# Last feed-forward of a two-layer diffusion backbone: second products two d_ff tiles behind, weight halves in another ring

## The chip, the cores and the metric

The kernel runs on one core of a Trainium2 chip. The metric is the time of one launch on the device, in microseconds (us). Five engines work side by side, each in the order of its own queue: TensorE (matrix products; PE in the profile, PEld its weight loads), VectorE (DVE), ScalarE (ACT), GpSimd (POOL) and SyncE (SP), which here issues nearly all transfers from memory. Engines wait for one another by semaphores only.

## The reference, cut to what matters

Two layers work on 256 latent tokens and 256 context tokens of width 1024. A layer is a half-step SwiGLU feed-forward, a token mixer, and another half-step feed-forward, each behind an RMS norm with a learned modulation. After the last layer only the latent tokens are normalised and returned. The change touches the last feed-forward and the final norm behind it:

```python
def rms_norm(x, g):
    y = xf * lax.rsqrt(jnp.mean(xf * xf, axis=-1, keepdims=True) + EPS)
    return y * g

def swiglu(h, w_in, w_out):                 # w_in 1024 x 5632, w_out 2816 x 1024
    g, u = jnp.split(h @ w_in, 2, axis=-1)
    return (jax.nn.silu(g) * u) @ w_out

x = x + 0.5 * mx[8] * swiglu(modulate(rms_norm(x, norm_g[layer, 2]), mx[6], mx[7]), w_in, w_out)
...
return rms_norm(x, final_norm_g)
```

Everything is float32 in the reference.

## The kernel before, in words

**Products in three passes.** A float32 operand is held as a pair: a high part, which is the value rounded to TensorE's fast float32 form by a copy on ScalarE, and a low part, which is the value less the high part, a subtraction on VectorE. `split` (L198, L199) makes the pair; `mm3` (L226 to L228) multiplies high by high, high by low and low by high into one PSUM bank. So each weight tile that comes from memory passes a raw buffer (`weight_raw`, L207), a copy and a subtraction, before TensorE can use it.

**Rings.** Buffers come from rings by tag. `raw` has 3 buffers of 1024 columns for fetched weights. `whi` and `wlo` have 4 each, also of 1024, for the parts of weights. `r2k` is the general ring: 46 buffers of 512 columns, from which activations and their parts come. PSUM has 8 banks. A buffer is given out again when its last reader is done; who gets which is settled when the program is built. A planner also settles the order of the instructions on each engine then: it goes by the program's order and lets a later instruction go first where it believes an earlier one not ready. On the chip each engine then keeps that order.

**The stage ahead.** The attention's output projection (`closing`, with one step for each of 8 blocks of 128 features) adds its result to the residual stream, and as each block of x is finished, `Raw.grown` splits it for the feed-forward (scaled by the norm's gain, without the token's rstd, which is applied to the products later) and adds its square to the sums. `Raw.leading` then multiplies the weights of the first d_ff tile, og and ou, and calls `rstd`: four tiny products of the sums with ones (L239), square root, reciprocal, two transposes (L245) and a copy (L247).

**The last feed-forward**, `last_ffn`, loops over 22 tiles f of 128 d_ff columns. In each step:

- the first products: og (gate) and ou (up), each 8 blocks in 3 passes, 24 products of 258 columns (256 tokens and two columns that carry the shift's product)
- the fetch of 128 rows of w_out (1024 columns, `in_woutn`), their multiplication by the output gate on GpSimd (L912), and their split into one `whi` and one `wlo` buffer
- the second products of an earlier tile, `second` (L906): two token blocks by two halves of 512 output columns by three passes, 12 products of 512 columns that add up in four PSUM banks over all f
- the activations of tile f: end columns copied (L918, L919), products times rstd (L921, L923), Silu (L922), sum and product (L924), and their split into two `r2k` buffers (L926, L927).

`held` is the list of tiles whose second products are to come. Before the change the loop empties it in each step, ahead of the step's own activations, so that the second products stand one tile behind, but step 20 leaves it alone; step 21 then does tiles 19 and 20, and tile 21 follows after the loop. In steps 5, 7, 9 and 11 the residual x is added to the four banks by products with the identity (L932). After the loop come the final norm's squares (L941), root, scaling and the two stores for each half of the tokens.

The raw buffers are asked for in the order og, ou, w_out of each tile, and SyncE issues the fetches in that order.

Of the kernel before, what the change touches and what calls it, by code (L numbers as in the profile page):

```python
# [19 lines left out]
KT = D // P  # L20
# [3 lines left out]
NF = DFF // P  # L24
# [13 lines left out]
def hybrid_backbone_kernel(ctx, tc, t, out):  # L38
    nc = tc.nc
# [5 lines left out]
    def bank(shape=(P, 512)):  # L45
        return ps.tile(list(shape), F32, tag="bank", name="bank")

    def r2k(n=512, parts=P):
        return ring.tile([parts, n], F32R, tag="r2k", name="r2k", bufs=46)

    def tmp(n=512, parts=P):
        return ring.tile([parts, n], F32, tag="tmp", name="tmp", bufs=6)
# [4 lines left out]
    def big():  # L57
        return ring.tile([P, 1152], F32R, tag="big", name="big", bufs=4)

    def small(n=4):  # L60
        return ring.tile([P, n], F32, tag="small", name="small", bufs=24)
# [28 lines left out]
    def behind(ins):  # L90

        return tc.issue_after(ins.ins) if ins else nullcontext()
# [102 lines left out]
    def split(hi, lo, src, bias=None, engine=nc.vector):  # L195

        if bias is None:
            nc.scalar.copy(hi, src)  # L198
            return engine.tensor_tensor(lo, src, hi.bitcast(F32), ALU.subtract)  # L199
        else:  # L200
            nc.scalar.activation(hi, src, AF.Identity, bias=bias)
            return nc.vector.scalar_tensor_tensor(lo, src, bias, hi.bitcast(F32), ALU.add, ALU.subtract)  # L202

    def weight_raw(ap, n=1024, raw=None):
        if raw is None:
            raw = ring.tile([P, 1024], F32, tag="raw", name="wraw", bufs=3)
        nc.sync.dma_start(raw[:, :n], ap)  # L207
        return raw[:, :n]
# [4 lines left out]
    def weight_split(raw, engine=nc.vector, after=None):  # L213
        n = raw.shape[1]
        hi = ring.tile([P, 1024], F32R, tag="whi", name="whi", bufs=4)
        lo = ring.tile([P, 1024], F32R, tag="wlo", name="wlo", bufs=4)
        with behind(after):
            split(hi[:, :n], lo[:, :n], raw, engine=engine)
        return hi[:, :n], lo[:, :n]

    def mm3(o, terms, which=None, n=None):

        n = n or len(terms)
        for i in range(n) if which is None else which:
            (ah, al), (bh, bl) = terms[i]
            nc.tensor.matmul(o, lhsT=ah, rhs=bh, start=(i == 0), stop=False)  # L226
            nc.tensor.matmul(o, lhsT=ah, rhs=bl, start=False, stop=False)  # L227
            nc.tensor.matmul(o, lhsT=al, rhs=bh, start=False, stop=(i == n - 1))  # L228
# [42 lines left out]
    class Sublayer:  # L271
# [61 lines left out]
        def leading(self, s):  # L333


            self.product(self.lead[:self.both], s)
            if len(self.streams) > 1 and s == 0:
                self.r[1] = self.rstd(1)
            for i in range(self.both, len(self.first)):
                if i == len(self.lead):  # L340
                    ap, size = self.first[i]
                    self.lead.append((weight(ap, size, after=self.end), bank(), size // KT))
                self.product(self.lead[i:i + 1], s)
# [65 lines left out]
    def ffn_specs(l, which):  # L409
        return [(t["win"][l, which, f, u], 1024) for f in range(NF) for u in range(2)]  # L410
# [422 lines left out]
    class Raw(Sublayer):  # L833
# [20 lines left out]
        def leading(self, s):  # L854
            for k in range(KT):
                for wt, o, M in self.lead:
                    mm3(o[:M, :self.W], self.terms(wt, M), (k,))
            _, self.r = self.rstd(s)

        def products(self, specs):  # L860
            for i, (ap, size) in enumerate(specs):
# [28 lines left out]
    def last_ffn(sl):  # L890


        fngr = big().bitcast(F32)[:, :1024]
        nc.sync.dma_start(fngr, t["fngr"])
        outs = sl.products(ffn_specs(1, 1))
        acc = [[bank() for _ in range(2)] for _ in range(2)]
        r = sl.r
        held = []

        def second(f, gu, w):  # L900
            for i in range(2):
                rows = slice(i * P, (i + 1) * P)
                for h in range(2):
                    cols = slice(h * 512, h * 512 + 512)
                    for j, (a, b) in enumerate(((0, 0), (0, 1), (1, 0))):
                        nc.tensor.matmul(acc[i][h], lhsT=gu[a][:, rows], rhs=w[b][:, cols],  # L906
                                         start=(f == 0 and j == 0), stop=(f == NF - 1 and j == 2))

        for f in range(NF):
            og, ou = next(outs), next(outs)  # L910
            raw = weight_raw(t["woutn"][f])
            nc.gpsimd.tensor_tensor(raw, raw, gate, ALU.mult)  # L912
            wt = weight_split(raw)

            while held and f != NF - 2:
                second(*held.pop(0))
            ends = small(2)
            nc.scalar.copy(ends[:, 0:1], og[:, T:T + 1])  # L918
            nc.scalar.copy(ends[:, 1:2], ou[:, T:T + 1])  # L919
            g, u = tmp(T), tmp(T)  # L920
            nc.vector.tensor_tensor(g, og[:, X], r, ALU.mult)  # L921
            nc.scalar.activation(g, g, AF.Silu, bias=ends[:, 0:1])  # L922
            nc.vector.tensor_tensor(u, ou[:, X], r, ALU.mult)  # L923
            nc.vector.scalar_tensor_tensor(u, u, ends[:, 1:2], g, ALU.add, ALU.mult)  # L924
            gu = (r2k(T), r2k(T))
            hi = nc.scalar.copy(gu[0], u)  # L926
            nc.vector.tensor_tensor(gu[1], u, gu[0].bitcast(F32), ALU.subtract)  # L927
            held.append((f, gu, wt))
            if f in (5, 7, 9, 11):
                i, h = (f - 5) // 4, (f - 5) // 2 % 2  # L930
                for d in range(4):
                    nc.tensor.matmul(acc[i][h][:, d * P:(d + 1) * P], lhsT=xs[4 * h + d][:, i * P:(i + 1) * P], rhs=ident,  # L932
                                     start=False, stop=False)
        with behind(hi):
            nc.scalar.activation(small(1), r[:, 0:1], AF.Sqrt)
        second(*held.pop())
        for i in range(2):
            sums, rs = small(2), small(1)
            ys = [tmp() for _ in range(2)]
            for h in range(2):  # L940
                nc.scalar.activation(ys[h], acc[i][h], AF.Square, accum_out=sums[:, h:h + 1])  # L941
            nc.vector.tensor_tensor(rs, sums[:, 0:1], sums[:, 1:2], ALU.add)
            nc.scalar.activation(rs, rs, AF.Sqrt, scale=1.0 / D, bias=eps)
            nc.vector.reciprocal(rs, rs)
            for h, queue in enumerate((nc.sync, nc.scalar)):
                cols = slice(h * 512, h * 512 + 512)
                if i == 0 and h == 1:
                    nc.scalar.activation(ys[h], acc[i][h], AF.Copy, scale=rs)
                    nc.gpsimd.tensor_tensor(ys[h], ys[h], fngr[:, cols], ALU.mult)
                else:  # L950
                    nc.vector.scalar_tensor_tensor(ys[h], acc[i][h], rs, fngr[:, cols], ALU.mult, ALU.mult)
                queue.dma_start(out[i, :, cols], ys[h])
# [107 lines left out]
    sl, nxt = nxt, Raw(1, 2, (0,), ffn_specs(1, 1)[:2])  # L1060
    swa(sl, nxt)
    last_ffn(nxt)


# [80 lines left out]
```

## Time and profile before

| | |
|---|---|
| median of 3 runs | 1699.57 us (1696.93 to 1700.79) |
| profiled execution, its own time | 1699.09 us |
| its span | 1697.3 us |
| TensorE busy | 1672.6 us, 99% of the span |
| VectorE busy | 1080.8 us, 64% |
| ScalarE busy | 645.4 us, 38% |
| GpSimd busy | 222.5 us, 13% |
| granted TensorE clock, mean | 0.999 |

The time of the profiled execution is its span and 1.79 us around it. A line of the profile names the line of the program that issued the instruction; a helper such as `split` has one line for all its callers, so the tiles written and read (out<-in) tell them apart: `wraw<-in_win` is a fetch of first-layer weights, `wraw<-in_woutn` one of the last w_out. In the timeline each row gives start and duration in us, the engine and line, the operation, the names and shapes, the count, and in brackets how long the engine had been idle before and what released it. A product's duration includes its passage through the array, so products overlap: their pace is read from the distance of their starts. The last feed-forward takes the last 200 us of the span.

### The profile page before, as it was taken

The numbers are of one execution on the slowest core, as the hardware profiler recorded it, in microseconds if no ns is written. First come the engines' busy times: TensorE is split into PE (matmuls) and PEld (weight loads), VectorE is DVE, ScalarE is ACT, GpSimd is POOL, SyncE is SP. The second block draws the span as 40 slices with busy tenths as digits, with TensorE's granted clock in tenths as the row PEclk, the third lists the DMA queues.
The fourth block names the chain that finished last, engine by engine and source line by source line (L and its number), as shares of the span: only waits on it lengthen the run. The fifth ranks groups of instructions, "written<-read, shape, count | busy, mean of one in ns | idle before, by whom it ended". The sixth has DMA issues, their size and how long they took to land.

```text
span 1697.3 us, 23433 instructions
## 1 busy us (share of the span) xinstructions
PE 1672.6 (99%) x9294; PEld 1417.5 (84%) x9294; DVE 1080.8 (64%) x1538; ACT 645.4 (38%) x1132; POOL 222.5 (13%) x186
## 2 busy tenths in 40 slices
PE   9999999999999999999999999999999999999997
PEld 7888878888788898788888897888888898789997
DVE  6776777645668568856847365644433367778886
ACT  4421322235556353222222353222222366654444
POOL 0000000004132130000000130000000253133332
PEclk9999999999999999999999999999999999999999
DMA  9655556531211126644645335735332222155553
GB/s 345 220 164 183 167 186 194 162 124 57 88 50 63 56 84 200 207 149 154 208 144 172 107 112 196 234 123 162 114 100 92 95 88 77 62 161 175 174 186 113
DMA packets 71536, 243.75 MB, mean 144 GB/s; under 512 B 8577, under 2 KB 9345, under 8 KB 71425
## 3 DMA queue, kind: packets, MB, share of 16 engines
q1 hardware_dynamic: 70560, 241.54, 43.7%
q8 instruction: 73, 1.20, 0.3%
q10 hardware_dynamic: 864, 0.70, 0.1%
q14 instruction: 39, 0.31, 0.1%
HBM read 241.16 MB, written 1.05 MB: 143 GB/s over the span
## 4 chain that ended last, share of the span: by engine, by line
PE 79%; DMA 5%; DVE 5%; ACT 4%; POOL 3%; issue 2%; ACTq 0%; DVEq 0%; SPq 0%; POOLq 0%
PE bank L226 25%; PE bank L227 25%; PE bank L228 24%; DMA wraw<-in_woutn 4%; POOL wraw L912 3%; DVE wlo L199 2%; ACT whi L198 2%; DMA r2k<-in_modo 1%; PE bank L177 1%; DVE big L171 1%; PE bank L239 1%; DVE small L454 0%; PE bank L482 0%; PE bank L906 0%; DMA modraw<-in_modw 0%
## 5 line engine op out<-in xcount | busy, mean ns | idle before, releaser
L226 PE MATMUL bank<-r2k,whi 128*128 128x512 f32 (+2 forms) x2434 | 866.7, 357 | 0.9 <-ACT small L918 0.9
L227 PE MATMUL bank<-r2k,whi 128*128 128x512 f32 (+2 forms) x2434 | 861.9, 354 | 2.6 <-DVE r2k L202 1.2
L228 PE MATMUL bank<-r2k,wlo 128*128 128x512 f32 (+2 forms) x2434 | 861.4, 354 | 1.1 <-DVE wlo L199 0.9
L198 ACT CAST whi<-wraw 128x1024 fp32r<-128x1024 f32 (+1 forms) x311 | 319.9, 1033 | 851.1 <-PE bank L227 502.1
L226 PEld LDWEIGHTS bank<-r2k,whi 128*128 128x128 f32 x2434 | 459.1, 189 | 79.5 <-ACT whi L198 9.2
L227 PEld LDWEIGHTS bank<-r2k,whi 128*128 128x128 f32 x2434 | 460.2, 189 | 68.4 <-DVE r2k L202 1.9
L228 PEld LDWEIGHTS bank<-r2k,wlo 128*128 128x128 f32 x2434 | 460.1, 189 | 65.8 <-DVE wlo L199 2.0
L199 DVE TENSOR_TENSOR wlo<-wraw,whi 128x1024 fp32r<-128x1024 f32 (+1 forms) x300 | 363.5, 1218 | 117.2 <-ACT whi L198 110.1
L171 DVE SCALAR_TENSOR_TENSOR big<-modraw,conds,big 128x1024 f32<-128x1024 f32 x189 | 233.3, 1278 | 14.7 <-DMA modraw<-in_modw 14.4
L264 POOL TENSOR_TENSOR strip<-strip 128x256 f32<-128x256 f32 x58 | 57.3, 1002 | 939.5 <-ACT strip L258 465.2
L366 DVE SCALAR_TENSOR_TENSOR x<-bank,mod,x 128x256 f32<-128x256 f32 x168 | 74.3, 478 | 154.0 <-PE bank L228 154.0
L428 DVE TENSOR_TENSOR tmp<-bank,tmp 128x512 f32<-128x512 f32 x66 | 45.6, 690 | 160.7 <-PE bank L228 158.1
L912 POOL TENSOR_TENSOR wraw<-wraw,gate 128x1024 f32<-128x1024 f32 x22 | 63.5, 2888 | 127.2 <-DMA wraw<-in_woutn 127.0
L906 PE MATMUL bank<-whi,r2k 128*128 128x512 f32 x176 | 58.0, 392 | 3.1 <-DVE r2k L927 1.8
L927 DVE TENSOR_TENSOR r2k<-tmp,r2k 128x256 fp32r<-128x256 f32 x22 | 51.0, 2318 | 0.9 <-ACT r2k L926 0.9
L199 DVE TENSOR_TENSOR r2k<-bank,r2k 128x512 fp32r<-128x512 f32 (+2 forms) x73 | 40.7, 593 | 16.1 <-ACT r2k L198 15.6
L199 DVE TENSOR_TENSOR r2k<-tmp,r2k 128x512 fp32r<-128x512 f32 x66 | 45.1, 684 | 1.4 <-ACT r2k L198 1.4
L198 ACT CAST r2k<-tmp 128x512 fp32r<-128x512 f32 x66 | 41.0, 622 | 12.8 <-DVE tmp L428 12.4
L454 DVE TENSOR_REDUCE small<-bank 128x1 f32<-128x512 f32 (+1 forms) x64 | 37.0, 614 | 7.4 <-PE bank L777 7.2
L906 PEld LDWEIGHTS bank<-whi,r2k 128*128 128x128 f32 x176 | 33.0, 188 | 10.2 <-DVE r2k L927 2.2
L426 ACT ACTIVATE tmp<-bank 128x512 f32<-128x512 f32 x66 | 38.9, 590 | 3.7 <-PE bank L228 3.7
L198 ACT CAST r2k<-bank 128x512 fp32r<-128x512 f32 (+2 forms) x73 | 34.4, 524 | 12.7 <-PE bank L228 8.8
(195 smaller groups left out, 1147.5 us busy)
## 6 DMA issues: line engine op xcount, KB each, us to landing
wraw<-in_win SPq DMA_DIRECT2D x172, 512.0 KB, 3.9
modraw<-in_modw SPq DMA_DIRECT2D x128, 512.0 KB, 4.2
wraw<-in_wout SPq DMA_DIRECT2D x48, 448.0 KB, 3.3
wraw<-in_wout SPq DMA_DIRECT2D x24, 512.0 KB, 4.4
wraw<-in_woutn SPq DMA_DIRECT2D x22, 512.0 KB, 3.5
r2k<-in_modo SPq DMA_DIRECT2D x32, 256.0 KB, 6.0
wraw<-in_mwo SPq DMA_DIRECT2D x8, 512.0 KB, 3.5
wraw<-in_swq SPq DMA_DIRECT2D x8, 512.0 KB, 3.5
```

Of the source, the lines that this page charges most:

```text
L171: nc.vector.scalar_tensor_tensor(acc[s], raw, conds[:, kt, s:s + 1], acc[s], ALU.mult, ALU.add)
L198: nc.scalar.copy(hi, src)
L199: return engine.tensor_tensor(lo, src, hi.bitcast(F32), ALU.subtract)
L226: nc.tensor.matmul(o, lhsT=ah, rhs=bh, start=(i == 0), stop=False)
L227: nc.tensor.matmul(o, lhsT=ah, rhs=bl, start=False, stop=False)
L228: nc.tensor.matmul(o, lhsT=al, rhs=bh, start=False, stop=(i == n - 1))
L264: nc.gpsimd.tensor_tensor(self.parts[0], self.parts[0], q, ALU.add)
L366: nc.vector.scalar_tensor_tensor(xs[d][:, SL[s]], o[:, SL[s]], mod[l][:, s, c:c + 1], xs[d][:, SL[s]], ALU.mult, ALU.add)
L428: nc.vector.tensor_tensor(pr[:, :w], ou[:, :w], sg[:, :w], ALU.mult)
L906: nc.tensor.matmul(acc[i][h], lhsT=gu[a][:, rows], rhs=w[b][:, cols], start=(f == 0 and j == 0), stop=(f == NF - 1 and j == 2))
L912: nc.gpsimd.tensor_tensor(raw, raw, gate, ALU.mult)
L927: nc.vector.tensor_tensor(gu[1], u, gu[0].bitcast(F32), ALU.subtract)
```

## The change

Three things. First, `second` is called one tile later: in step f when more than one tile is held, so for tile f - 2, in every step from 2 on; what is left (tiles 20 and 21) is done after the loop. Step 20 is no exception any more. Second, the gated w_out rows are no longer split as one tile of 1024 columns into `whi` and `wlo`, but as two halves of 512 columns, each into two buffers of `r2k`; `second` takes half h as its operand. Third, in `Raw.leading` the sums for rstd are asked for after the last block of og, ahead of the last three products of ou, and no longer after both.

```diff
@@ Raw.leading
             for k in range(KT):
                 for wt, o, M in self.lead:
                     mm3(o[:M, :self.W], self.terms(wt, M), (k,))
-            _, self.r = self.rstd(s)
+                    if k == KT - 1 and wt is self.lead[0][0]:
+                        _, self.r = self.rstd(s)
@@ last_ffn, second
                 for h in range(2):
-                    cols = slice(h * 512, h * 512 + 512)
                     for j, (a, b) in enumerate(((0, 0), (0, 1), (1, 0))):
-                        nc.tensor.matmul(acc[i][h], lhsT=gu[a][:, rows], rhs=w[b][:, cols],
+                        nc.tensor.matmul(acc[i][h], lhsT=gu[a][:, rows], rhs=w[h][b],
                                          start=(f == 0 and j == 0), stop=(f == NF - 1 and j == 2))
@@ last_ffn, the loop
             raw = weight_raw(t["woutn"][f])
             nc.gpsimd.tensor_tensor(raw, raw, gate, ALU.mult)
-            wt = weight_split(raw)
-
-            while held and f != NF - 2:
+            wt = [(r2k(), r2k()) for _ in range(2)]
+            for h in range(2):
+                split(*wt[h], raw[:, h * 512:h * 512 + 512])
+            if len(held) > 1:
                 second(*held.pop(0))
@@ last_ffn, after the loop
-        second(*held.pop())
+        for h in held:
+            second(*h)
```

## The prediction

> **What bounds the kernel now.** I read the page first, for the span, and then only the stage of the last feed-forward. It has 22 tiles of d_ff. For tile f, TensorE does 48 first products (og and ou, 24 each, 258 columns; I call them p f) and 12 second products (512 columns; s f). The order on TensorE now is p0 p1 s0 p2 s1 ... p19 s18 p20 p21 s19 s20 s21.
>
> ```profile
> span 1697.3 us, 23433 instructions
> ```
>
> The execution took 1699.09 us, so 1.79 lie outside the span. The second view is the timeline of TensorE (start, duration, line, operation, and in brackets the idle time and who ended it).
>
> ```profile
> 1503.33 0.28 PE L228 MATMUL bank<-r2k,wlo 128*128 128x258 f32 x1
> 1504.93 0.50 PE L906 MATMUL bank<-whi,r2k 128*128 128x512 f32 x1 [1.32 <-ACT small L919]
> ...
> 1508.39 1.20 PE L906 MATMUL bank<-whi,r2k 128*128 128x512 f32 x4 [1.80 <-DVE r2k L927]
> ...
> 1509.88 0.28 PE L226 MATMUL bank<-r2k,whi 128*128 128x258 f32 x1
> ...
> 1526.88 0.28 PE L226 MATMUL bank<-r2k,whi 128*128 128x258 f32 x1
> ...
> 1532.63 0.40 PE L906 MATMUL bank<-whi,r2k 128*128 128x512 f32 x1
> ...
> 1535.38 0.28 PE L226 MATMUL bank<-r2k,whi 128*128 128x258 f32 x1
> ...
> 1672.30 0.28 PE L228 MATMUL bank<-r2k,wlo 128*128 128x258 f32 x1
> 1673.44 0.39 PE L226 MATMUL bank<-r2k,whi 128*128 128x258 f32 x1 [0.86 <-ACT small L918]
> ...
> 1674.89 0.39 PE L228 MATMUL bank<-r2k,wlo 128*128 128x258 f32 x1 [0.95 <-DVE wlo L199]
> ...
> 1682.06 0.39 PE L906 MATMUL bank<-whi,r2k 128*128 128x512 f32 x1
> ```
>
> In the middle TensorE is full: p lasts 1532.63 - 1526.88 = 5.75 us (0.12 a product), s lasts 1535.38 - 1532.63 = 2.75, a tile 8.50. Only two places lose time. **The first** is s0: p1 ends at 1503.33 + 0.12 = 1503.45 and s0 begins at 1504.93, 1.48 us later; then it takes 1509.88 - 1504.93 = 4.95 in place of 2.75, 2.20 more, as it waits for the low half of its own tile's activations (L927). Together 3.68. **The second** is p21: p20 ends at 1672.42 and s19 begins at 1682.06, so p21 takes 9.64 in place of 5.75, 3.89 more. The two waits in brackets are 1.81 of it. Most of the rest is the clock, by the windows view (the four busy times, then the granted clock):
>
> ```profile
> 1497.00:1510.00 13.00, 9.88 (x69) 8.80 (x68) 10.14 (x13) 7.11 (x15) 3.87 (x2) 1.00 0.53 163
> ...
> 1675.30:1678.50 3.20, 3.20 (x17) 3.20 (x16) 2.67 (x4) 1.82 (x4) 1.04 (x1) 0.50 0.34 124
> ```
>
> After the waits at 1673 TensorE ran 3.2 us at half speed; after the waits at 1504 it did not. The sum of both places is 3.68 + 3.89 = 7.57 us, 0.45% of the time. That is all that an order of work in this stage can win, for TensorE's own work is the same before and after.
>
> Why p21 is late is told by the chain of waits (start, duration, engine and line):
>
> ```profile
> 1654.75 1.24 DVE wlo L199
> 1656.01 3.45 DMA wraw<-in_woutn
> 1659.59 2.93 POOL wraw L912
> 1662.54 1.06 ACT whi L198
> 1663.62 1.24 DVE wlo L199
> 1664.87 3.52 DMA wraw<-in_woutn
> ...
> 1674.89 0.39 PE bank L228
> ```
>
> This is a loop through one raw buffer: second-layer weights of a tile are fetched, multiplied by the gate on GpSimd, copied (high part) on ScalarE, subtracted (low part) on VectorE, and only then may the next tile's fetch start. It takes 1663.62 - 1654.75 = 8.87 us a tile, more than TensorE's 8.50. TensorE therefore eats its lead and meets the loop at the end. The first-layer fetches stand behind this fetch in SyncE's queue, so they come at the same pace.
>
> **The change, part by part.** TensorE's order becomes p0 p1 p2 s0 p3 s1 ... p20 s18 p21 s19 s20 s21. Every s f for f below 19 moves behind one more p; the end from p21 on is the same, and before p21 stands the same work as now.
>
> *The lag at the start.* s0 now starts after p2, at 1503.45 + 5.75 = 1509.20 at the earliest. What it waited for is there by then: L927 released it at 1508.39. So 3.68 go, if p2 has its weights in time. What shows this is the next group of rows, from the timelines of VectorE, GpSimd and ScalarE.
>
> ```profile
> 1504.61 1.23 DVE L199 TENSOR_TENSOR wlo<-wraw,whi 128x1024 fp32r<-128x1024 f32 x1 [0.26 <-ACT whi L198]
> ...
> 1504.64 3.41 POOL L912 TENSOR_TENSOR wraw<-wraw,gate 128x1024 f32<-128x1024 f32 x1 [7.19 <-DMA wraw<-in_woutn]
> ...
> 1510.14 1.05 ACT L198 CAST whi<-wraw 128x1024 fp32r<-128x1024 f32 x1 [0.44 <-PE bank L906]
> ...
> 1684.92 0.42 DVE L927 TENSOR_TENSOR r2k<-tmp,r2k 128x256 fp32r<-128x256 f32 x1 [0.47 <-ACT r2k L926]
> ```
>
> The subtraction at 1504.61 is that of ou2: ready at 1505.84, wanted at 1503.45 + 24 x 0.12 = 1506.33. So p2 has it with 0.5 us to spare, now, and this term is worth between 3.68 (no wait) and 0 (p2 so late that s0 is not displaced). I take 3.68, as the weights can only come earlier, by the next part.
>
> *The weight halves in the general ring.* The four whi and four wlo buffers, now shared by two first-layer and one second-layer tile for each f, are left to the first layer: two whole tiles of lead. The row at 1510.14 prices one wait that goes: tile 2's gated weights were ready at 1504.64 + 3.41 = 1508.05, but the copy started 2.09 us later, when s0 (L906) had given a buffer back. In the changed kernel nothing there waits for s0. The loop for tiles 3 to 20 then starts 2.09 earlier (0 if ScalarE or VectorE is busy with something else then, no row gives more).
>
> The split itself becomes two copies and two subtractions. The nearest rows are the 512-column splits elsewhere:
>
> ```profile
> L927 DVE TENSOR_TENSOR r2k<-tmp,r2k 128x256 fp32r<-128x256 f32 x22 | 51.0, 2318 | 0.9 <-ACT r2k L926 0.9
> L199 DVE TENSOR_TENSOR r2k<-bank,r2k 128x512 fp32r<-128x512 f32 (+2 forms) x73 | 40.7, 593 | 16.1 <-ACT r2k L198 15.6
> L199 DVE TENSOR_TENSOR r2k<-tmp,r2k 128x512 fp32r<-128x512 f32 x66 | 45.1, 684 | 1.4 <-ACT r2k L198 1.4
> L198 ACT CAST r2k<-tmp 128x512 fp32r<-128x512 f32 x66 | 41.0, 622 | 12.8 <-DVE tmp L428 12.4
> ```
>
> As work it adds 2 x 0.62 - 1.06 = 0.18 us on ScalarE and 2 x 0.68 - 1.24 = 0.12 on VectorE for a tile, 22 times, none on TensorE. As latency, from the end of the gating to the free raw buffer, it is now 1664.87 - 1662.54 = 2.33. The second copy can run under the first subtraction: 0.62 + 2 x 0.68 = 1.98, a gain of 0.35 and a loop of 8.52. If all four run one after another it is 2 x 0.62 + 2 x 0.68 = 2.60, a loop of 9.14. I take 8.52, since the two engines alternate in that way in the present splits.
>
> *What that makes of the end.* og21's split now ends at 1674.85 (the product at 1674.89 waits for it), 9.98 after the fetch of tile 20's second-layer weights at 1664.87. In the changed kernel that fetch comes 2.09 + 17 x 0.35 = 8.0 earlier, at 1656.8, and og21 is ready at 1666.8. p21 wants it at 1672.42 - 3.68 = 1668.74: 1.9 us to spare. So the wait at p21 goes and does not come back though TensorE arrives earlier, and with it the slow clock: 3.89. With the loop at 8.87 there would be a wait; that is the first rival.
>
> *After p21* nothing is new: now L927 of tile 21 ends at 1684.92 + 0.42 = 1685.34, 3.28 after p21's end, and s19 and s20 cover 5.50 of TensorE. Without that cover it would cost the 3.28; the cover stays. What would be late next is tile 21's second-layer weights, and those have the whole of p21, s19 and s20, 11.25 us.
>
> *rstd's sums higher.* They are moved ahead of the last three of 48 products, so 3 x 0.12 = 0.36 earlier; their chain ends in tile 0's activations, which have p2 in front of them now. Taken at nothing: at best 0.36, at worst 0.36 back if their inputs are not there, both covered by the 5.75 of p2. Without p2 there the 0.36 would be s0's.
>
> Sum: 1699.09 - 3.68 - 3.89 = 1691.5. The median of the runs shown, 1699.57, lies 0.48 above the profiled execution; I put the time at 1691.7, between the two bases.
>
> **The rivals.** *The loop keeps its pace.* If the split in halves gains nothing, the fetch is only 2.09 earlier, og21 is ready at 1672.8, and p21 waits 4.0 us. The half-speed stretch comes again (p21's 3.89 less the waits of 1.81 is 2.08, with edges). That is 6.1 back: 1697.8. For it speaks that the loop has set this end for over 100 us; against it that a copy and a subtraction of half the size are on two engines.
>
> *A wait of some 2 us is left at the start*, where p2 has only 0.5 to spare, or s0 meets L927, which takes 2.318 on average and 0.42 when GpSimd is quiet. Then the time is 1693.7, and 1695.8 with the clock's 2.08. The Trainium skill's page "TensorE: Matmul & The Clock Gate", section "Why this matters for your kernels", says that only idle gaps above about 3 us bring the slow clock; by it 1693.7 would hold. The trace agrees at 1504 and disagrees at 1673, where gaps of 0.86 and 0.95 were enough, so I leave both.
>
> *Slower:* the two halves are torn apart on VectorE. If a first-layer subtraction (1.24) is queued between them in each tile, the loop is 8.52 + 1.24 = 9.76. Starting 2.09 earlier, tile 20's fetch comes at 1664.87 - 2.09 + 17 x (9.76 - 8.87) = 1677.9, og21 at 1687.9, 19.2 after p21 wants it: 1691.5 + 19.2 + 2.1 = 1713. It turns to a loss where wait and clock exceed 7.57, so a wait of 5.5, og21 at 1674.2: a loop above 8.87 + (1674.2 - 1672.8) / 17 = 8.95. For it: VectorE works in order, and a subtraction waits for its copy. Against: the second copy is done while the first half is subtracted, so there is no time for another to get between. The Trainium skill ("SBUF — State Buffer", "SBUF: two separate sides") adds that VectorE and GpSimd lock each other out of a shared port for a whole instruction when VectorE reads two operands from SBUF; L927's 2.318 against 0.42 agrees. By that rule halves that meet GpSimd would stretch, but the next gating is fetched only after them.
>
> *It doesn't do what it says:* the planner runs s0 ahead of p2 again because it believes p2's weights late. Then the start gains nothing and the end does: 1695.2. It goes with the second rival.
>
> **How the numbers follow.** No waits left: 0.60, 1691.7, its own range 1690 to 1693. A wait at the start or the start not gained: 0.15, 1693.7 to 1695.8. The loop keeps its pace: 0.17, 1697.8. Torn halves: 0.08, to 1713. A measurement of this kernel tells about 0.2%, 3.4 us: faster is below 1696.2, slower above 1703. Faster: the first two and a little of the third, where the gain is in part there, 0.78. Same: 0.15. Slower: 0.07. The range runs from 1689.5 (the first case, less 2.2, about what the lowest run lies under the median) to 1697.5, which leaves out the last case and half of the third.
>
> **What would show it.** Right: TensorE's products in this stage have no wait above 0.3 us between p1 and s21; L906 first appears after p2; the granted clock stays 1.00 up to the last product; the interval between GpSimd's gatings is at most 8.6 where TensorE does not hold it back. Wrong: a wait of p20 or p21 for L199 with half clock behind it (the loop), a wait ahead of p2 or s0 (the start), or subtractions of a whole first-layer tile between two halves (torn).

## The result, and the profile after

The changed kernel takes 1714.07 us (median of 4 runs, 1713.08 to 1714.50), the kernel before 1698.25 in the same session: a ratio of 1.0089, 95% interval 1.0073 to 1.0105. It is some 15 us slower (15.1 by the ratio, 15.8 by the medians), where 7.6 us of gain were forecast. The profiled execution took 1713.99 us.

First the span, and what TensorE waited for in the stage (engine and line, released by, total us, times, longest):

```profile
span 1712.2 us, 23496 instructions
```

```profile
PE bank L226 <- DVE tmp L924: 6.1, 6, 1.5
PE bank L228 <- DVE wlo L199: 4.6, 7, 0.8
PE bank L906 <- ACT r2k L927: 1.9, 2, 1.2
PE bank L245 <- DVE small L242: 1.0, 1, 1.0
PE bank L226 <- DVE tmp L922: 0.6, 1, 0.6
```

(The edit moves lines: L922, L924, L925, L927 and L928 are now what L921, L923, L924, L926 and L927 were. L199 stays the low half of a split.) The second products are hardly waited for; the first products are, for the low half of their weights (L228) and for a PSUM bank that the activations of an earlier tile have not yet emptied (L226 behind L924). The windows view of two stretches, columns as before (length, busy TensorE, its weight loads, VectorE, ScalarE, GpSimd, granted clock):

```profile
1530.00:1583.00 53.00, 53.00 (x379) 50.01 (x379) 34.72 (x44) 22.25 (x44) 15.15 (x6) 1.00 0.51 169
1583.00:1694.00 111.00, 100.53 (x672) 90.33 (x672) 76.62 (x87) 44.47 (x88) 28.12 (x11) 1.00 0.48 152
```

From 1530 to 1583 TensorE runs full, on the lead from the start and the identity products. Then it waits about once in each tile, and stands still for 10.5 of the next 111 us. The chain of waits shows for what:

```profile
1665.03 3.44 DMA wraw<-in_win
1668.51 0.04 issue
1668.55 1.05 ACT whi L198
1669.62 1.23 DVE wlo L199
1670.85 0.34 DVE tmp L924
1671.22 0.50 DVE tmp L925
1671.74 0.41 ACT r2k L927
1672.18 2.07 DVE r2k L928
...
1674.77 0.69 DVE r2k L199
1675.49 0.03 issue
1675.52 3.41 DMA wraw<-in_win
1678.95 1.06 ACT whi L198
1680.03 1.23 DVE wlo L199
1681.25 0.34 DVE r2k L928
1681.59 3.42 DVE r2k L199 x2
1685.03 0.03 issue
1685.06 3.56 DMA wraw<-in_win
```

This is not the loop of the kernel before. There the fetch of second-layer weights (`in_woutn`) and the gating were in it. Now the fetch of *first-layer* weights (`in_win`) is, their split, the activations' instructions, and then the two halves of second-layer weights (r2k L199), after which the next first-layer fetch may start. Two tiles take 1685.06 - 1665.03 = 20.03 us, 10.0 a tile, against TensorE's 8.50.

Why does a first-layer fetch wait for second-layer halves? They share the raw buffers. Tile 20's weights can be followed through the timelines of SyncE, GpSimd and VectorE:

```profile
1676.74 0.33 SPq L207 DMA_DIRECT2D wraw<-in_woutn  x1
...
1681.66 2.79 POOL L912 TENSOR_TENSOR wraw<-wraw,gate 128x1024 f32<-128x1024 f32 x1 [7.69 <-DVE r2k L928]
...
1685.77 1.23 DVE L199 TENSOR_TENSOR wlo<-wraw,whi 128x1024 fp32r<-128x1024 f32 x1 [0.44 <-ACT whi L198]
1689.79 1.23 DVE L199 TENSOR_TENSOR wlo<-wraw,whi 128x1024 fp32r<-128x1024 f32 x1 [2.79 <-ACT whi L198]
...
1694.34 1.28 DVE L199 TENSOR_TENSOR r2k<-wraw,r2k 128x512 fp32r<-128x512 f32 x2
```

They are fetched at 1676.74 and gated by 1684.45, but the halves come only at 1694.34: the splits of og21 and ou21 (the two whole tiles) and the activations of tile 19 stand ahead of them in VectorE's order. The raw buffer is occupied from 1676.74 to 1695.62, 18.9 us. In the kernel before, VectorE takes the low half of the same weights directly ahead of that of og21 (the pair below; the second of the two starts at 1673.62), so the buffer is occupied from 1664.87 to 1673.62, 8.75 us:

```profile
1672.48 2.36 DVE L199 TENSOR_TENSOR wlo<-wraw,whi 128x1024 fp32r<-128x1024 f32 x2 [0.83 <-ACT whi L198]
```

At 10 us a tile, in the changed kernel, nearly two of the three raw buffers hold second-layer weights, and the first layer's two tiles pass through what is left, one after the other.

### The profile page after: what moved, and what is told of

It is laid out like the page before. It is cut to its first block, busy times and chain, and to the rows that moved or that the text cites. A ratio compares the mean times of both kernels' runs of the same rounds, so it can differ in the third digit from the quotient of the medians.

```text
span 1712.2 us, 23496 instructions
## 1 busy us (share of the span) xinstructions
PE 1679.2 (98%) x9294; PEld 1417.9 (83%) x9294; DVE 1070.0 (62%) x1560; ACT 646.3 (38%) x1154; POOL 214.3 (13%) x186
## 4 chain that ended last, share of the span: by engine, by line
PE 79%; DVE 8%; DMA 5%; ACT 5%; issue 2%; POOL 1%; SPq 0%; ACTq 0%; DVEq 0%; POOLq 0%
PE bank L226 25%; PE bank L227 25%; PE bank L228 24%; DMA wraw<-in_win 4%; DVE r2k L199 2%; DVE wlo L199 2%; ACT whi L198 2%; DVE r2k L928 1%; PE bank L177 1%; DVE tmp L925 1%; DVE small L454 0%; PE bank L482 0%; PE bank L239 0%; DMA c_ng<-in_ng 0%; ACT r2k L198 0%
## 5 line engine op out<-in xcount | busy, mean ns | idle before, releaser
L226 PE MATMUL bank<-r2k,whi 128*128 128x512 f32 (+2 forms) x2434 | 867.4, 357 | 7.0 <-DVE tmp L924 6.1
L228 PE MATMUL bank<-r2k,wlo 128*128 128x512 f32 (+2 forms) x2434 | 862.1, 355 | 4.8 <-DVE wlo L199 4.6
L198 ACT CAST whi<-wraw 128x1024 fp32r<-128x1024 f32 (+1 forms) x289 | 298.2, 1033 | 854.5 <-PE bank L227 493.0
L226 PEld LDWEIGHTS bank<-r2k,whi 128*128 128x128 f32 x2434 | 458.3, 189 | 88.0 <-ACT whi L198 9.2
L228 PEld LDWEIGHTS bank<-r2k,wlo 128*128 128x128 f32 x2434 | 459.2, 189 | 71.6 <-DVE wlo L199 7.6
L199 DVE TENSOR_TENSOR wlo<-wraw,whi 128x1024 fp32r<-128x1024 f32 (+1 forms) x278 | 337.8, 1217 | 141.8 <-ACT whi L198 134.9
L912 POOL TENSOR_TENSOR wraw<-wraw,gate 128x1024 f32<-128x1024 f32 x22 | 55.4, 2517 | 148.6 <-DMA wraw<-in_woutn 66.9
L906 PE MATMUL bank<-r2k 128*128 128x512 f32 x264 | 64.6, 393 | 1.9 <-ACT r2k L927 1.9
L906 PEld LDWEIGHTS bank<-r2k 128*128 128x128 f32 x264 | 47.7, 188 | 12.7 <-ACT r2k L927 3.1
L199 DVE TENSOR_TENSOR r2k<-bank,r2k 128x512 fp32r<-128x512 f32 (+2 forms) x73 | 40.7, 593 | 17.4 <-ACT r2k L198 16.9
L199 DVE TENSOR_TENSOR r2k<-tmp,r2k 128x512 fp32r<-128x512 f32 x66 | 45.2, 684 | 1.4 <-ACT r2k L198 1.4
L199 DVE TENSOR_TENSOR r2k<-wraw,r2k 128x512 fp32r<-128x512 f32 x44 | 39.0, 922 | 5.0 <-ACT r2k L198 4.6
```

The costliest lines, as they stand in the source:

```text
L906: nc.tensor.matmul(acc[i][h], lhsT=gu[a][:, rows], rhs=w[h][b], start=(f == 0 and j == 0), stop=(f == NF - 1 and j == 2))
```

## The experiments

**Theory A**: with `whi` and `wlo` free for the first layer, the planner pulls both first-layer splits of tile f + 1 ahead of the halves of tile f, and the raw buffer kept so long starves the first layer. **Theory B**: the halves themselves are the load, two for one and blocked by GpSimd's gating (L199 on a half took 893 ns on average in this stage). **Theory C**: the lag is the load. All runs with their ratio to the kernel before on the same chip:

| run | what | us (median) | ratio, 95% interval |
|---|---|---|---|
| changed kernel | all | 1714.07 | 1.0089 (1.0073 to 1.0105) |
| e1_lag_alone | lag | 1710.52 | 1.0065 (1.0050 to 1.0080) |
| e2_halves_alone | halves | 1717.93 | 1.0101 (1.0069 to 1.0132) |
| e3_raw4 | all, 4 raw buffers | 1692.08 | 0.9953 (0.9938 to 0.9968) |
| e4_order | all, splits put in order | 1694.79 | 0.9967 (0.9957 to 0.9978) |
| e5_fill | all, gating left out | 1692.72 | 0.9962 (0.9947 to 0.9977) |
| e6_before_raw4 | kernel before, 4 raw buffers | 1695.89 | 0.9984 (0.9974 to 0.9993) |
| e7_halves_raw4 | halves, 4 raw buffers | 1694.40 | 0.9970 (0.9961 to 0.9979) |
| e8_raw4_no_rstd | all but rstd, 4 raw buffers | 1692.67 | 0.9962 (0.9947 to 0.9977) |
| e9_lag_raw4 | lag, 4 raw buffers | 1718.28 | 1.0114 (1.0097 to 1.0131) |
| e10_raw4_order | all, 4 raw buffers, in order | 1697.22 | 0.9988 (0.9978 to 0.9997) |

### The lag alone

```diff
-            while held and f != NF - 2:
+            if len(held) > 1:
                 second(*held.pop(0))
@@ after the loop
-        second(*held.pop())
+        for h in held:
+            second(*h)
```

> Only the lag of two tiles; the second-layer weights are split whole into whi and wlo as before, rstd's sums where they were. Theory A (order and raw buffers: with whi and wlo free for the first layer, the planner puts both first-layer splits of tile f+1 ahead of the second-layer halves of tile f, so a raw buffer stays occupied for a tile longer and the two others feed a loop of 10.1 us a tile): the order of splits stays as before, no such loop, not slower than 1700. Theory B (the lock between VectorE and GpSimd: halves take 0.92 us each because they meet the gating): no halves, so also not slower than 1700. Theory C (the lag itself, which keeps activations and weights longer): near 1714.

1710.52: theory A's number here was wrong. Its waits:

```profile
ACT whi L198 <- PE bank L906: 17.5, 17, 1.2
PEld bank L228 <- DVE wlo L199: 17.4, 17, 1.5
PE bank L228 <- DVE wlo L199: 14.0, 17, 1.3
```

A copy into `whi` waits, once in nearly every tile, for second products (L906) to give a buffer back, and TensorE waits 14.0 us for weights behind it. By the program, with a lag of two, tiles f - 2 and f - 1 hold two of the four buffers and p f's own weights the other two. So the lag needs the other ring (e9_lag_raw4 below bears on that again); that does not say that theory C explains the changed kernel, where the waits are different ones.

### The halves alone

```diff
-            wt = weight_split(raw)
+            wt = [(r2k(), r2k()) for _ in range(2)]
+            for h in range(2):
+                split(*wt[h], raw[:, h * 512:h * 512 + 512])
```

> Only the halves in the general ring; second products one tile behind with the old exception, rstd's sums where they were. Theory A: the loop of 10.1 us a tile is there, 1708 to 1718. Theory B: the halves meet the gating, the same 1708 to 1718. Theory C: near 1698.

1717.93, over a wide spread of 1709.97 to 1722.14. Part of this time is the clock: the mean granted clock was 0.996 in the fastest of its four runs and 0.993 in the slowest, which is the profiled one, against 0.998 in the changed kernel. TensorE waits in another place, since the second products are still one tile behind and reach the late activations first:

```profile
PE bank L906 <- DVE r2k L929: 8.2, 5, 2.7
PE bank L906 <- ACT r2k L928: 6.6, 5, 2.2
```

What releases it (L928 and L929 are the high and low half of the activations in this kernel) stands in the same order behind the first-layer splits, and its chain of waits runs through first-layer fetches and halves as the changed kernel's does. So the slow loop comes with the halves in the general ring, without the lag: theory C falls, A and B both stand.

### A fourth raw buffer, and the order by hand

```diff
-            raw = ring.tile([P, 1024], F32, tag="raw", name="wraw", bufs=3)
+            raw = ring.tile([P, 1024], F32, tag="raw", name="wraw", bufs=4)
```

> The changed kernel with four raw buffers in place of three, nothing else. Theory A: the occupied raw buffer no longer starves the first layer, the waits of TensorE for L199 and for the banks go, 1689 to 1696. Theory B: VectorE and GpSimd block each other as much as before, 1708 to 1716.

1692.08, 7.9 under the kernel before on the same chip, and so about the time forecast for the change itself. TensorE's groups in the last stage (columns: busy, mean ns, idle before) show no wait at all; below them the halves and the low part of the activations on VectorE:

```profile
L226 PE MATMUL bank<-r2k,whi 128*128 128x258 f32 (+1 forms) x370 | 105.1, 284 | 0.0
L228 PE MATMUL bank<-r2k,wlo 128*128 128x258 f32 (+1 forms) x371 | 105.0, 283 | 0.0
...
L906 PE MATMUL bank<-r2k 128*128 128x512 f32 x264 | 63.7, 391 | 0.0
```

```profile
L199 DVE TENSOR_TENSOR r2k<-wraw,r2k 128x512 fp32r<-128x512 f32 x42 | 36.0, 891 | 0.3 <-ACT r2k L198 0.2
L928 DVE TENSOR_TENSOR r2k<-tmp,r2k 128x256 fp32r<-128x256 f32 x22 | 35.7, 1622 | 0.9 <-ACT r2k L927 0.9
```

The halves take 891 ns as in the changed kernel, so they are held up by the gating about as much, and it costs TensorE nothing. Theory B as a load of its own falls.

The other way to give raw buffers back in time is the order. The first-layer splits of the next tile are tied behind the halves:

```diff
+                    with behind(self.copied), behind(self.end):
-                    wt = weight(ap, size)
+                        wt = weight(ap, size)
@@ last_ffn
-                split(*wt[h], raw[:, h * 512:h * 512 + 512])
+                half = raw[:, h * 512:h * 512 + 512]
+                sl.copied = nc.scalar.copy(wt[h][0], half)
+                sl.end = nc.vector.tensor_tensor(wt[h][1], half, wt[h][0].bitcast(F32), ALU.subtract)
```

> The changed kernel, with the first-layer splits of tile f+1 put behind the halves of tile f on ScalarE and on VectorE by hand; three raw buffers. Theory A: raw buffers are given back in the order in which they were fetched, the loop of 10.1 us goes, 1690 to 1700. Theory B: the halves are still two for one and still share VectorE's port with the gating, 1708 or more.

1694.79, within what theory A gave. From tile 3 on TensorE has no wait; in p2 it loses 2.2 us to first-layer copies that now stand behind halves. The blocking has not gone: it now falls on the sum and product of the activations (L929 in this kernel), which takes 2.06 us on average here and 0.49 in e5_fill below, and TensorE has no wait from it. Three raw buffers are enough here if they are emptied in the order in which they are filled.

### The loop and the lock

```diff
-            nc.gpsimd.tensor_tensor(raw, raw, gate, ALU.mult)
+            nc.gpsimd.memset(raw, 0.01)
```

> The changed kernel (three raw buffers) with the gating left out: in its place GpSimd fills the same buffer with a constant, so it reads nothing from SBUF; the order of the splits on VectorE is the same as in the changed kernel. If the loop through the occupied raw buffer is long enough by itself, the time stays at 1708 or more. If it is the loop and the lock together (two tiles of the loop take 20.1 us in the changed kernel; without the 2.1 that the halves and the 1.7 that the low half of the activations wait for the gating they take about 16.3, so 8.2 a tile, less than TensorE's 8.50), TensorE is the bound again: 1690 to 1696.

1692.72. The three rows that differ from the changed kernel:

```profile
L199 DVE TENSOR_TENSOR r2k<-wraw,r2k 128x512 fp32r<-128x512 f32 x42 | 27.2, 685 | 3.4 <-ACT r2k L198 2.5
...
L912 POOL MEMSET wraw<- 128x1024 f32 x20 | 19.1, 955 | 154.7 <-DMA wraw<-in_woutn 94.0 <-DVE r2k L928 22.8 <-DVE tmp L925 13.3
L928 DVE TENSOR_TENSOR r2k<-tmp,r2k 128x256 fp32r<-128x256 f32 x22 | 9.3, 421 | 5.3 <-ACT r2k L927 5.2
```

In the chain of the changed kernel L928 took 2.07 and the halves 3.42 in alternate tiles; here 0.42 and two times 0.685. The order of the splits is that of the changed kernel, and tile 20's raw buffer is still occupied for 15 us (1658.31 to 1673.26). So theory A needs an addition: the new loop is longer than TensorE's tile only *with* the blocking in it. Either the free raw buffer or the order (the loop is cut), or the free port (the loop is short), makes TensorE the bound again. One thing goes with the edit: the fill is also shorter than the gating, 0.96 us against some 2.5. The trace speaks against that as the cause. From 1530 on the copies of the halves start 3.6 us or more after their fill has ended, so a gating 1.5 us longer would not have held them up; and where a fill runs over the subtractions, they take no longer than alone:

```profile
1564.56 1.28 DVE L199 TENSOR_TENSOR r2k<-wraw,r2k 128x512 fp32r<-128x512 f32 x2
1564.73 0.95 POOL L912 MEMSET wraw<- 128x1024 f32 x1 [7.28 <-DVE r2k L928]
```

### What each part is worth with four raw buffers

The kernel before, and the changed kernel without one part, each with the edit of e3_raw4 on top.

> The kernel before with four raw buffers and nothing of the change. If its end is set by one raw buffer's loop alone, p21's wait and the slow clock go and s0's wait stays: 1695 to 1697. If whi and wlo hold the first layer back at the end as well, nothing moves: 1698 to 1701.

1695.89. p21's wait and the half-speed stretch are gone, s0's wait is the only one left:

```profile
PE bank L906 <- ACT small L919: 2.3, 1, 2.3
```

So the prediction read the end of the kernel before rightly: one raw buffer's loop set it.

> Halves in the general ring and four raw buffers, second products still one tile behind. If the lag is worth what s0 and the later second products wait for, 1695 to 1699; if four raw buffers and free whi are the whole gain, 1692, as the changed kernel with four raw buffers.

1694.40, a little better than expected; TensorE still waits 1.1 us ahead of s0. The lag is worth 1.7 us on top of it (1692.67 in the next run, which differs from this one in the lag alone); the intervals of the two ratios overlap, so the size is uncertain.

> The changed kernel with four raw buffers, rstd's sums back behind the first products. If moving them up is worth nothing, 1692, as with them moved; if it is what lets p1 and p2 run through, 1693 to 1695.

1692.67 against 1692.08 on another chip, and the intervals of the two ratios overlap for the most part: moving rstd's sums is worth nothing that shows.

> Only the lag of two tiles, second-layer weights whole in whi and wlo, and four raw buffers. If the lag alone is slow because three second-layer tiles hold three of the four whi and wlo buffers, a fourth raw buffer doesn't help: 1706 to 1712. If it is slow for want of raw buffers as the changed kernel is, 1692 to 1697.

1718.28, a miss by 6 but on the side expected. The copies into `whi` now wait for first products:

```profile
ACT whi L198 <- PE bank L227: 53.1, 20, 3.8
```

A raw buffer is no cure where the parts' buffers are short; it made this case 8 us worse, and TensorE's waits for the low half of first-layer weights grew from 14.0 to 19.9 us. Why worse was not followed up.

> The changed kernel with four raw buffers and the splits put in order by hand. With four raw buffers TensorE has no wait left in the stage's loop, so the order has nothing to give: within 2 of the changed kernel with four raw buffers alone, 1691 to 1695. If the order counted for itself, under 1690.

1697.22, a miss: 5 us slower than four raw buffers without the order. Nearly all of the loss is ahead of p3: s0 ends at 1517.1, in e3_raw4 at 1512.5. Of these 4.6 us, 1.5 are there when p0 starts (1492.84 against 1491.32), ahead of this stage, and stay unexplained. The rest is in p2, where the order leaves the first-layer splits too late:

```profile
1506.90 0.39 PE L226 MATMUL bank<-r2k,whi 128*128 128x258 f32 x1 [1.19 <-ACT whi L198]
1507.84 0.39 PE L226 MATMUL bank<-r2k,whi 128*128 128x258 f32 x1 [0.43 <-ACT whi L198]
1511.83 0.39 PE L228 MATMUL bank<-r2k,wlo 128*128 128x258 f32 x1 [0.60 <-DVE wlo L199]
```

The lowest time is that of e3_raw4 (e8_raw4_no_rstd lies within its interval): the change with a fourth raw buffer beats both kernels, by 0.5% the one before.

## Why the prediction was wrong

**Right**: that TensorE loses time at s0 and at p21 only, what the two cost together, and why p21 was late. With four raw buffers both losses go, and the kernel is 7.9 us under the one before on the same chip, where the sum gave 7.57. The end of s19 to s21 needs no new wait there (in the changed kernel itself s20 and s21 wait 1.9 us for late activations). rstd's sums at nothing holds there too.

**Wrong** is one step, in "The lag at the start", in the part on the weight halves and in "What that makes of the end". It says that the whi and wlo buffers left to the first layer can only bring its weights earlier, and that og21 is ready 9.98 us after the fetch of tile 20's second-layer weights, as before. Both took the order of the instructions on ScalarE and VectorE as fixed. It was not. In the kernel before, the second-layer split stands ahead of the first-layer splits of the next tile; with the halves in the other ring, two first-layer splits stand ahead of it, and the raw buffer that was occupied for 8.75 us is occupied for 18.9. That the planner had held the first-layer splits back because they had no free whi and wlo buffer fits this, but what the planner believed is not shown. The loop of 8.52 that the prediction gave to the second-layer fetch became one of 10.0 through the first-layer fetch, which the prediction had at the same pace "behind this fetch in SyncE's queue". From 1583 on it costs TensorE more than the start gained. The blocking by the gating, which the prediction set aside, is the other half of this loop: with the same order and without it (e5_fill) the kernel takes 1692.72.

**The start** was right in size. Of the 3.68 the changed kernel shows 1.8 (p2 and s0 are done at 1513.88 in place of 1515.63). Its p0 starts 0.7 later than in the kernel before (1491.48 against 1490.76), ahead of this stage, and some 1.2 go in p1, which stands still for 1.0 until the reciprocal of rstd is there; that stands on VectorE behind the low half of a whole first-layer tile. The same wait, 1.04, is in e2_halves_alone, where rstd's sums are not moved. With four raw buffers s0 is done at 1512.51, 3.1 earlier, though p0 starts 0.56 later: 3.68 within the stage.

**The rivals**: the torn halves have the time, 1713, and not the mechanism, so that the number agrees is luck. In the timeline of VectorE above, the two halves stand together (x2, 1.28); what comes ahead of them is the two first-layer tiles whole, and the loop that grows is another. "The loop keeps its pace" is wrong in sign. For the sentence that speaks for the lock, the trace agrees as far as it goes: halves that meet the gating do stretch, to 3.42 a pair. The argument set against it, that the next gating is fetched only after them, fell: with halves this late the next tile's weights are already in another raw buffer, and are being gated, at that moment (from 1681.66, while the halves of tile 19 run from 1681.59).

## What to carry to other kernels

When buffers are freed in a kernel whose order a planner sets, ask what the planner will pull forward, and which *other* ring the work pushed back keeps occupied: here parts' buffers were freed and raw buffers paid. Where several streams share a ring, check the order of fetches against the order of the last readers, tile by tile, before adding up gains: three raw buffers were enough when emptied in the order in which they were filled, and not when emptied out of it beside the gating. One more buffer of 4 KB a partition in the ring that became short turned a loss of 0.9% into a gain of 0.5%; without the change it gained 0.16%.

## What was not expected of the hardware

VectorE's subtraction of 128x256 between two SBUF operands took 421 ns on average beside a GpSimd fill that reads nothing, 1093 beside the gating in the changed kernel and 1622 with four raw buffers. The Trainium skill's rule on the shared port ("SBUF — State Buffer", "SBUF: two separate sides") names reading GpSimd instructions, and the fill agrees with that. The clock: in the changed kernel TensorE had gaps of up to 1.5 us, mostly some 10 us apart, and the granted clock stayed at 1.00 over 111 us; in the kernel before, gaps of 0.86 and 0.95 within 2.6 us were followed by half speed. In e2_halves_alone gaps of 1.13 and 1.35 within 3.3 us were followed by half speed, and gaps of 0.51 and 1.48 within 2.8 us were not. The Trainium skill's advice to have no idle gaps above about 3 us ("TensorE: Matmul & The Clock Gate", "Why this matters for your kernels") would have all of these be harmless; this holds for some and not for the others, and what tells them apart stays open.
